# ScalarE's scans of weight rows are put behind the first rounding of the loop's weights in a hybrid encoder layer

## The chip, the core and the metric

The kernel runs on one core of a Trainium2 chip. A core has a matrix engine, TensorE (PE in the profile, with its weight loads as PEld); three engines for elementwise work, VectorE (DVE), ScalarE (ACT) and GpSimd (POOL); and SyncE (SP), which here only issues transfers. All work at the same time, each on its own queue of instructions in a fixed order, and wait for each other by semaphores. Data lie in the on-chip memory, in tiles of 128 partitions; matrix products are written to a separate accumulator memory (PSUM). The metric is the time of one launch in microseconds on the device; lower is better.

## The reference

The reference computes one encoder layer for 1024 tokens of width 1024 in 32-bit floating point. A normalised input goes through one projection into two mixers (windowed grouped-query attention, and a two-dimensional neighbourhood attention); their outputs are normalised, concatenated and projected. What matters here is the second half, a gated block with a short convolution:

```python
hn = rmsnorm(h, norm_ffn)
g = einsum('bsd,df->bsf', hn, w_gate)          # 1024 -> 2816
u = einsum('bsd,df->bsf', hn, w_up)
g = conv3(g) * conv_w + conv_b                 # depthwise, over the tokens
h = h + einsum('bsf,fd->bsd', silu(g) * u, w_down)
out = rmsnorm(h, norm_final)
```

## The kernel before

The 2816 hidden columns are cut into 22 units of 128, taken in an order `FO`. For each unit the products with the gate and the up weights are formed together by a Strassen-like scheme: seven products of half size, named `p1` to `p7` in the class `Gated`, of weight blocks and their sums ("11", "12", "s1" to "s4", "22") with activations prepared once. Each product is made in 16-bit parts: a 32-bit operand is rounded to a 16-bit value `whi`, and what the rounding lost is kept as `wlo`. `group` (lines 1173 to 1177) then issues three matrix instructions for each of four depth blocks, `whi` twice and `wlo` once, so a product is 12 of them. `split_w` (lines 1145 to 1152) makes the two parts: ScalarE rounds (line 1150), VectorE subtracts (line 1151). Both multiply by a scale, a power of two `m`, so that the values fit 16 bits.

The scale of a unit comes from its weights, so they are read twice. First a **scan**: `scan_rows` (lines 1159 to 1164) loads a whole block of 512 KB (384 KB for some blocks of the down weights) into one of two `scan` buffers, through SyncE's queue, and ScalarE squares it and sums along each row (an activation, and a second short instruction that reads the sum). `settle_scales` (lines 1021 to 1035) takes the row sums of up to four units: VectorE adds gate and up (`wv`, line 1027), TensorE transposes so that all partitions see all rows (`wm`, line 1009), VectorE takes the maximum (line 1011) and turns it into `m` (lines 243 to 245) and its inverse (line 1030). Later `load_raw` loads the same weights again, and `split_w` rounds them with `m`.

The first four units are the **head**. Their products are issued product by product: all four units' `p1` and `p2`, then `p5`, `p6`, `p3`, `p7` and `p4`. While the head runs, ten scans are traced: two for each of the next four units, and two for the one after. At the head's end stands a short loop over its four units: `p4` of each, and with each of them three steps of `Weights`, the object that prepares the next unit's weights. The first three steps are `load` (it settles the scales and loads), `w11` and `w12`, the first two roundings for the first unit of the loop.

The **loop over units** (from line 1594) then runs over the other 18. In each turn it forms the seven products of its unit, and between them its helper `more` takes one step of the next unit's `Weights` and one step of `scanning`. The latter are the loop's scans: two for the unit five places ahead, and two of the 24 scans of the down weights, whose scale is needed at the end of the loop. In all there are 60 scans: ten in the head and 50 in the loop.

After the loop the products with the down weights follow, by the same scheme, and then the final normalisation.

What sets the order of the work: TensorE's instructions are kept in the order in which the program lists them. Those of the other engines, and the transfers, are ordered when the kernel is built, by a planner that simulates the engines: of the instructions whose inputs and buffers are ready in its simulation it takes the one of highest priority, normally the one listed first. `tc.high_priority(offset=...)` moves an instruction ahead in that. It can therefore put an instruction of a later turn of the loop well ahead of where it is listed, where an engine is free in its simulation. Once built, each queue's order is fixed. `behind(names)` adds an edge of order, without a semaphore, that puts an instruction later in its engine's queue than the marked one.

## Time and profile before

| What | Value |
|---|---|
| median of 3 runs | 1040.5 us (1039.18 to 1040.81) |
| profiled execution | 1043.51 us |
| its span, first to last instruction | 1041.7 us |
| mean granted TensorE clock | 0.994 |
| TensorE busy | 1014.5 us (97%) |
| VectorE busy | 879.5 us (84%) |
| ScalarE busy | 678.3 us (65%) |
| GpSimd busy | 213.2 us (20%) |
| scans on ScalarE | 60, 61.2 us, from 380.1 to 612.7 us |
| transfers | 191.28 MB, mean 184 GB/s |

How to read the lines: in a timeline a line has the start and the length in us, the engine, the line of the kernel, the instruction with what it writes and reads, its count, and in brackets the idle time of its engine before it and what ended that. In the list of waits, a line has who waited for whom, the time in total, the number of times and the longest. In the view by stages a line has the stage and its length, the busy time of each engine in it (PE, PEld, DVE, ACT, POOL, with counts), the granted TensorE clock as a share of full speed, the share of the transfer engines' time that was used, and GB/s; where the view is of one line of the kernel, it has that line's engine alone. In the list of groups a line has the busy time and the mean length of one instruction in ns, then the idle time before them. The lengths of matrix instructions overlap, so their pace is read from their starts.

### The profile page before, as it was taken

The numbers are of one execution on the slowest core, as the hardware profiler recorded it, in microseconds if no ns is written. First come the engines' busy times: TensorE is split into PE (matmuls) and PEld (weight loads), VectorE is DVE, ScalarE is ACT, GpSimd is POOL, SyncE is SP. The second block draws the span as 40 slices with busy tenths as digits, with TensorE's granted clock in tenths as the row PEclk, the third lists the DMA queues.
The fourth block names the chain that finished last, engine by engine and source line by source line (L and its number), as shares of the span: only waits on it lengthen the run. The fifth ranks groups of instructions, "written<-read, shape, count | busy, mean of one in ns | idle before, by whom it ended". The sixth has DMA issues, their size and how long they took to land.

```text
span 1041.7 us, 15699 instructions
## 1 busy us (share of the span) xinstructions
PE 1014.5 (97%) x5098; PEld 577.9 (55%) x5098; DVE 879.5 (84%) x1748; ACT 678.3 (65%) x1243; POOL 213.2 (20%) x341
## 2 busy tenths in 40 slices
PE   8998999999999999999999999999999999999996
PEld 6776777777775545544344444444444444444446
DVE  6689998766898799899898888888888889899875
ACT  7557787767687587778777765445544656555551
POOL 2225455676866301000000000000000000000002
PEclk9999999999999999999999999999999999999998
DMA  9437574776699775564787752323323678877744
GB/s 347 152 93 147 111 131 85 156 166 141 134 179 224 217 271 195 158 189 149 239 260 251 251 185 91 122 91 122 112 101 112 226 258 303 297 247 258 260 152 162
DMA packets 144276, 191.28 MB, mean 184 GB/s; under 512 B 77377, under 2 KB 88641, under 8 KB 144193
## 3 DMA queue, kind: packets, MB, share of 16 engines
q1 hardware_dynamic: 133536, 164.51, 55.4%
q10 hardware_dynamic: 10656, 25.76, 6.4%
q8 instruction: 40, 0.66, 0.3%
q14 instruction: 44, 0.35, 0.1%
HBM read 132.81 MB, written 28.57 MB: 155 GB/s over the span
## 4 chain that ended last, share of the span: by engine, by line
PE 66%; DVE 5%; DMA 4%; ACT 4%; issue 1%; ACTq 0%; POOL 0%; DVEq 0%; POOLq 0%
PE dn L1177 6%; PE dn L1175 6%; PE dn L1176 6%; PE pj L180 6%; PE z L1176 4%; PE z L1177 4%; PE z L1175 4%; PE x L1177 3%; PE x L1176 3%; PE x L1175 3%; PE y L1175 3%; PE y L1176 3%; PE y L1177 3%; PE pj L172 2%; PE pj L174 2%; PE pj L173 2%
## 5 line engine op out<-in xcount | busy, mean ns | idle before, releaser
L1175 PEld LDWEIGHTS <-whi 128*128 128x128 f16 x898 | 88.2, 98 | 103.0 <-ACT whi L1150 2.6
L1177 PEld LDWEIGHTS <-wlo 128*128 128x128 f16 x898 | 88.0, 98 | 102.2 <-issue 0.8
L1176 PEld LDWEIGHTS <-whi 128*128 128x128 f16 x898 | 88.0, 98 | 100.6 <-issue 0.7
L1177 PE MATMUL dn<-xd,wlo 128*128 128x512 f16 (+1 forms) x330 | 120.4, 365 | 0.0
L1176 PE MATMUL dn<-xd,whi 128*128 128x512 f16 (+1 forms) x330 | 120.4, 365 | 0.0
L1175 PE MATMUL dn<-xd,whi 128*128 128x512 f16 (+1 forms) x330 | 120.4, 365 | 0.0
L172 PE MATMUL pj<-xgh,whi 128*128 128x512 f32 x248 | 107.3, 433 | 0.7 <-ACT whi L156 0.7
L1175 PE MATMUL z<-hg,whi 128*128 128x512 f16 x264 | 100.1, 379 | 0.0
L1176 PE MATMUL z<-hg,whi 128*128 128x512 f16 x264 | 100.1, 379 | 0.0
L1177 PE MATMUL z<-hg,wlo 128*128 128x512 f16 x264 | 100.1, 379 | 0.0
L174 PE MATMUL pj<-xgh,wlo 128*128 128x512 f32 x248 | 98.3, 396 | 1.4 <-POOL wlo L157 1.4
L466 ACT ACTIVATE p<-p,nm 128x385 f32<-128x385 f32 (+3 forms) x128 | 74.7, 584 | 38.0 <-DVE nm L462 33.3
L173 PE MATMUL pj<-xgl,whi 128*128 128x512 f32 x248 | 97.9, 395 | 0.0
L1150 ACT ACTIVATE whi<-ws,m 128x512 f16<-128x512 f32 (+1 forms) x96 | 65.6, 708 | 33.9 <-DVE ws L1316 26.4
L1151 DVE SCALAR_TENSOR_TENSOR wlo<-ws,m,whi 128x512 f16<-128x512 f32 (+1 forms) x96 | 70.1, 739 | 17.6 <-ACT whi L1150 17.4
L1031 POOL TENSOR_TENSOR back<-back,cst 128x4 f32<-128x4 f32 (+1 forms) x7 | 2.3, 335 | 362.4 <-DVE back L1030 362.4
L1164 ACT ACTIVATE scan<-scan 128x1024 f32<-128x1024 f32 (+1 forms) x60 | 61.2, 1019 | 18.8 <-DMA scan<-in_w_down_dram 8.9
L1151 DVE SCALAR_TENSOR_TENSOR wlo<-raw,m,whi 128x512 f16<-128x512 f32 (+1 forms) x78 | 55.1, 730 | 7.4 <-ACT whi L1150 7.4
L1175 PE MATMUL y<-hg,whi 128*128 128x512 f16 x160 | 60.9, 381 | 0.0
L1176 PE MATMUL y<-hg,whi 128*128 128x512 f16 x160 | 60.8, 380 | 0.0
L1177 PE MATMUL y<-hg,wlo 128*128 128x512 f16 x160 | 60.6, 379 | 0.0
L1578 DVE SCALAR_TENSOR_TENSOR xd<-xd,m 128x512 f16<-128x512 f32 x77 | 55.0, 745 | 6.0 <-ACT xd L1577 6.0
(291 smaller groups left out, 2458.7 us busy)
## 6 DMA issues: line engine op xcount, KB each, us to landing
xd<-x SPq DMA_DIRECT2D x77, 256.0 KB, 5.3
raw<-in_w_down_dram SPq DMA_DIRECT2D x64, 256.0 KB, 3.8
x<-c ACTq DMA_DIRECT2D x22, 512.0 KB, 2.8
scan<-in_w_gate_dram SPq DMA_DIRECT2D x18, 512.0 KB, 4.4
scan<-in_w_up_dram SPq DMA_DIRECT2D x18, 512.0 KB, 4.3
raw<-in_w_gate_dram SPq DMA_DIRECT2D x18, 512.0 KB, 3.5
raw<-in_w_up_dram SPq DMA_DIRECT2D x18, 512.0 KB, 3.5
raw<-in_w_in_dram SPq DMA_DIRECT2D x32, 256.0 KB, 3.3
```

Of the source, the lines that this page charges most:

```text
L172: nc.tensor.matmul(ps, w[0], x[0][:, tsl(h)], start=first, stop=False)
L173: nc.tensor.matmul(ps, w[0], x[1][:, tsl(h)], start=False, stop=False)
L174: nc.tensor.matmul(ps, w[1], x[0][:, tsl(h)], start=False, stop=last)
L180: nc.tensor.matmul(ps, a, b, start=i == 0 and b is x[h][0] and a is w[0], stop=i == len(ws) - 1 and a is w[1])
L466: nc.scalar.activation(p[:, 0:e], p[:, 0:e], AF.Exp, bias=nm, scale=-1.0, accum_out=sm)
L1150: nc.scalar.activation(hi, src, AF.Copy, scale=by)
L1151: nc.vector.scalar_tensor_tensor(lo, src, by, hi, op0=ALU.mult, op1=ALU.subtract)
L1164: nc.scalar.activation(t, t, AF.Square, accum_out=dst)
L1175: nc.tensor.matmul(ps, w[0], x[0], start=first and i == 0, stop=False, skip_group_check=True)
L1176: nc.tensor.matmul(ps, w[0], x[1], start=False, stop=False, skip_group_check=True)
L1177: nc.tensor.matmul(ps, w[1], x[0], start=False, stop=last and i == len(ws) - 1, skip_group_check=True)
L1578: nc.vector.scalar_tensor_tensor(lo, t[:, HALF:S], by, hi, op0=ALU.mult, op1=ALU.subtract)
```

## The change

The second rounding of the loop's first unit (`w12`, the last of the three steps taken in the first turn of the short loop at the head's end) is remembered as `first`. From then on, `scan_rows` puts ScalarE's squaring behind it in ScalarE's queue. The ten scans traced in the head are traced before the mark is set and carry no such edge; the 50 of the loop do. The edge is one of order in ScalarE's queue only. Instructions and transfers are the same.

```diff
             hi = fpool.tile([128, n, 128], F16, name="whi", tag="wh", bufs=9, padded_shape=pad)
             lo = fpool.tile([128, n, 128], F16, name="wlo", tag="wl", bufs=9, padded_shape=pad)
-            nc.scalar.activation(hi, src, AF.Copy, scale=by)
+            mark["whi"] = nc.scalar.activation(hi, src, AF.Copy, scale=by)
             nc.vector.scalar_tensor_tensor(lo, src, by, hi, op0=ALU.mult, op1=ALU.subtract)
...
             with behind(*["unit"] * ("unit" in mark)):
                 nc.sync.dma_start(t, src)
-            nc.scalar.activation(t, t, AF.Square, accum_out=dst)
+            with behind(*["first"] * ("first" in mark)):
+                nc.scalar.activation(t, t, AF.Square, accum_out=dst)
...
             u.p4()
             with tc.high_priority(offset=200):
                 w_next.step(3)
+            if i == 0:
+                mark["first"] = mark["whi"]
             if i < 2:
                 units[i + 2].conv()
```

## The prediction

> **What bounds the kernel now.** I read the page first, for the engine that sets the time.

> ```profile
> PE 1014.5 (97%) x5098; PEld 577.9 (55%) x5098; DVE 879.5 (84%) x1748; ACT 678.3 (65%) x1243; POOL 213.2 (20%) x341
> L1164 ACT ACTIVATE scan<-scan 128x1024 f32<-128x1024 f32 (+1 forms) x60 | 61.2, 1019 | 18.8 <-DMA scan<-in_w_down_dram 8.9
> ```

> TensorE (PE) is busy for 97% of the span, so time can only come from its gaps and from stretches in which its clock is low. ScalarE (ACT) has 60 scans, and before some of them it stands idle until their data land: 18.8 us in all. Then I asked who TensorE waits for from 470 to 640 us, which holds the end of the head and the loop's first units.

> ```profile
> PE x L1175 <- ACT whi L1150: 2.1, 1, 2.1
> PE x L1177 <- DVE wlo L1151: 0.2, 1, 0.2
> ```

> There are two waits and no other. The first is the change's own object: the first product of the loop's first unit waits for the rounded weights `whi`. TensorE's timeline shows the place, and a view by stages gives the granted clock (the column after the engines):

> ```profile
> 495.50 0.38 PE L1176 MATMUL z<-hg,whi 128*128 128x512 f16 x1
> 495.71 0.38 PE L1177 MATMUL z<-hg,wlo 128*128 128x512 f16 x1
> 498.19 0.39 PE L1175 MATMUL x<-hg,whi 128*128 128x512 f16 x1 [2.09 <-ACT whi L1150]
> 498.41 0.38 PE L1176 MATMUL x<-hg,whi 128*128 128x512 f16 x1
> 498.97 0.39 PE L1177 MATMUL x<-hg,wlo 128*128 128x512 f16 x1 [0.18 <-DVE wlo L1151]
> ...
> 500.35 0.63 PE L1176 MATMUL x<-hg,whi 128*128 128x512 f16 x1
> 500.78 0.63 PE L1177 MATMUL x<-hg,wlo 128*128 128x512 f16 x1
> ...
> 503.48 0.38 PE L1175 MATMUL y<-hg,whi 128*128 128x512 f16 x1
> ```

> ```profile
> 490.00:496.00 6.00, 6.00 (x29) 2.55 (x26) 6.00 (x12) 3.62 (x7) 0.00 (x0) 1.00 0.62 203
> 499.50:503.40 3.90, 3.90 (x12) 1.43 (x11) 3.90 (x7) 2.76 (x6) 0.00 (x0) 0.56 0.66 243
> 512.00:612.00 100.00, 100.00 (x467) 45.56 (x465) 88.67 (x129) 77.63 (x129) 1.19 (x5) 1.00 0.75 246
> 612.00:712.00 100.00, 100.00 (x469) 45.85 (x468) 85.58 (x128) 48.04 (x70) 3.48 (x10) 1.00 0.31 109
> ```

> Starts of neighbouring products lie 0.215 to 0.22 us apart at clock 1.00 (495.50 to 495.71) and 0.43 apart in the stage whose clock is 0.56 (500.35 to 500.78). So the gap costs twice: by itself, and by the slow clock behind it. The sum, at 0.216 us a product: the x product was due at 495.93 and started at 498.19, **2.26 us** late. From 498.19 to 503.48 are 15 products (12 of x, 3 of y) in 5.29 us, where 15 x 0.216 = 3.24 would do: **2.05 us** more, of which 0.34 is the wait for `wlo` (498.41 to 498.97 is 0.56) and 1.71 the slow clock. Together **4.31 us** hang on one late rounding. From 512 on TensorE is busy 100 of 100 us.

> **Why `whi` is late.** ScalarE's timeline ahead of it:

> ```profile
> 491.61 1.06 ACT L1164 ACTIVATE scan<-scan 128x1024 f32<-128x1024 f32 x1 [1.24 <-DMA scan<-in_w_down_dram]
> 492.67 1.04 ACT L1385 ACTIVATE cv<-cv 128x1024 f32<-128x1024 f32 x1
> 493.95 1.06 ACT L1164 ACTIVATE scan<-scan 128x1024 f32<-128x1024 f32 x1 [0.25 <-DMA scan<-in_w_gate_dram]
> 496.37 1.06 ACT L1164 ACTIVATE scan<-scan 128x1024 f32<-128x1024 f32 x1 [1.27 <-DMA scan<-in_w_up_dram]
> 497.42 1.32 ACT L1150 ACTIVATE whi<-raw,m 128x512 f16<-128x512 f32 x2
> ```

> The scans stand in the queue ahead of the two roundings, and wait for transfers. The last one, for a later unit's up weights, starts at 496.37 and lets `whi` go at 497.42. The scale `m`, which `whi` also needs, comes from VectorE (DVE):

> ```profile
> 465.90 0.75 DVE L1151 SCALAR_TENSOR_TENSOR wlo<-ws,m,whi 128x512 f16<-128x512 f32 x1 [2.14 <-ACT whi L1150]
> 471.70 0.75 DVE L1151 SCALAR_TENSOR_TENSOR wlo<-ws,m,whi 128x512 f16<-128x512 f32 x1 [1.31 <-ACT whi L1150]
> 491.83 0.68 DVE L1011 TENSOR_REDUCE m<-wm 128x4 f32<-128x512 f32 x1
> 495.02 0.16 DVE L245 TENSOR_SCALAR m<-m 128x4 f32<-128x4 f32 x1
> 495.14 1.28 DVE L1397 SCALAR_TENSOR_TENSOR c<-c,back,cv 128x1024 f32<-128x1024 f32 x1
> 496.34 0.17 DVE L1030 RECIPROCAL back<-m 128x4 f32<-128x4 f32 x1
> 498.16 1.41 DVE L1151 SCALAR_TENSOR_TENSOR wlo<-raw,m,whi 128x512 f16<-128x512 f32 x2 [1.65 <-ACT whi L1150]
> 503.15 0.74 DVE L1151 SCALAR_TENSOR_TENSOR wlo<-ws,m,whi 128x512 f16<-128x512 f32 x1
> ```

> `m` is done at 495.18 (495.02 + 0.16). So 2.24 us pass between the moment the data allow `whi` and its start, all of it in scans.

> **The change, part by part.** It adds an edge of order on ScalarE alone: each of the loop's 50 scans (60 less the ten traced in the head) comes behind the second rounding of the loop's first unit. No instruction or transfer is added, and an order inside one queue costs no instruction. The head's ten scans keep their places. How many are moved:

> ```profile
> 433.00:498.00 65.00, 24.37 (x44) 1.00 0.56 171
> 498.00:613.00 115.00, 30.43 (x56) 0.99 0.74 246
> ```

> Each scan is two instructions, so 44 in the upper row are 22 scans, the eleventh to the thirty-second: all 22 leave the head, with 24.4 us of ScalarE's time. With only two scan buffers, two of them can be loaded early; the loads of the others on SP's queue move behind the roundings as well.

> (1) *The roundings.* Behind the last `cv` (492.67 + 1.04) ScalarE has nothing left ahead of `whi`, which then starts when `m` is there. Lower bound of the gain: `m` stays at 495.18, `whi` starts at about 495.25, and with the 0.77 us of now (497.42 to 498.19) the product starts at 496.02, 0.09 late. `wlo` would still stand behind VectorE's 495.14 and 496.34 rows, which end at 496.51; with 0.81 from its start to the product (498.16 to 498.97), the third product starts at 497.32 where 496.45 was due, 0.87 late. Gain 4.31 - 0.09 - 0.87 = 3.35, if the clock holds. Then the fourth set of weights, `wlo` of z (503.15, now 1.65 earlier: 501.50 + 0.81 = 502.31), meets a product due at 497.32 + 24 x 0.216 = 502.50: it fits, by 0.2 us. Upper bound: VectorE too is held up in the head, 2.14 + 1.31 us by a `whi` that stood behind scans which waited for transfers; that gone, its queue, otherwise full, reaches row 491.83 up to 3.45 us earlier, `m` is done near 491.7, ahead of TensorE's need, and all 4.31 come back. I take **4.0**, nearer the upper end, since VectorE has no other long wait there and what it does in that stretch has its inputs.

> (2) *Does the clock hold?* Stalls of 0.09 and 0.87 are left at worst. Two other gaps of this trace bracket them:

> ```profile
> 372.29 1.02 PE L180 MATMUL pj<-mg,wo 128*128 128x512 f16 x4 [1.34 <-DVE mg L1123]
> 61.94 0.50 PE L174 MATMUL pj<-xgh,wlo 128*128 128x512 f32 x1 [1.37 <-POOL wlo L157]
> 374.00:378.00 4.00, 4.00 (x21) 1.99 (x20) 4.00 (x8) 4.00 (x8) 0.00 (x0) 1.00 0.80 319
> 64.00:68.00 4.00, 4.00 (x16) 3.23 (x15) 2.99 (x12) 1.09 (x4) 0.49 (x1) 0.72 0.32 99
> 59.83 0.50 PE L172 MATMUL pj<-xgh,whi 128*128 128x512 f32 x1 [0.66 <-ACT whi L156]
> ```

> One gap of 1.34 us left the clock at 1.00; 0.66 and 1.37 within some 2 us (2.03 together) were followed by 0.72. 0.96 lies below both, so I count the clock as full. [...]

> (3) *The moved scans.* 22 scans of 1.1 us join those of the loop. In 115 us the loop now runs 28, 4.1 us each; at that pace the 50 end near 496 + 50 x 4.1 = 701 instead of 613. The cover is the loop's idle ScalarE: 77.6 of 100 us busy with scans at this pace (512 to 612), 48.0 without (612 to 712), and TensorE without a gap in both. The load of the first stage now lasts into the second; transfers rise there from 109 to about 246 GB/s, which the first stage bore. Price **0**. Without that cover it would be 24.4 us.

> (4) *What is late next.* The scales of units nine to twelve need the loop's tenth scan. Their transposes have a fixed place in TensorE's order:

> ```profile
> 552.04 0.60 PE L1009 MATMUL wm<-cst,wv 128*128 128x128 f32 x4
> 491.16 0.15 DVE L1027 TENSOR_TENSOR wv<-w_rows 128x4 f32<-128x4 f32 x1
> ```

> Now `wv` is there 61 us ahead. After the change the tenth scan ends near 496 + 10 x 4.1 = 537, and TensorE asks at 552.04 - 4.3 = 547.7: some 10 us of slack remain. Price 0.

> Sum: 4.0 less. The profiled execution takes 1043.5 (span 1041.7 and 1.8 around it) and becomes 1039.5; it lies 3.0 above the median of the runs, 1040.5, so for them **1036.5**.

> **Rivals.**
> *The clock still falls* (0.13): the gap shrinks but a short stall is left, at `wlo` or at z, where the fit was 0.2 us, and a slow stretch like the present one follows. For it: the 0.72 after only 2.03 us. Against: 1.34 without a fall. Gain 3.35 - 1.71 = 1.6 to 2.6: 1037.9 to 1038.9.
> [...]
> *It doesn't do what it says* (0.07): something else takes the scans' place ahead of `whi`, or the scales arrive 2 us later in a new order of VectorE's queue. The rows speak against it, since only `cv` work is left there. Nothing moves: 1040.5.
> *Slower* (0.12): the scans now start late and their transfers come more slowly than now. From 5.2 us a scan on, the tenth misses 547.7, TensorE stands at the transposes, and every later product with it. At 5.6 us it ends at 552, and behind one queued step of VectorE (1.28) and `wv` (0.15) TensorE goes on near 553.5: 5.8 lost, 1.7 more by the clock, less the 4.0 won: 3.5 slower, 1044.0. For it: waits for transfers before 16 scans, 18.8 us of idleness. Against: the loop has sustained 4.1 with the same two buffers.
> *More than 4.31* (0.06): other waits of the new order fall away, 1035.

> **How the numbers follow.** The forecast case, gain 3.35 to 4.31, has 0.62: 1036.2 to 1037.2, widened by the spread of the runs (1.6) to 1035.4 to 1038. What a measurement of this kernel can tell from no change is about 0.2%, 2.1 us. Faster: 0.62 + 0.06 + half of 0.13, 0.75. Same: the other half and 0.07, 0.13. Slower: 0.12. The range 1034.8 to 1040.9 takes in the forecast, the faster end, the clock rival and a part of the unmoved case, and leaves out the slower one.

> **What would show it.** In the profile after: no scan on ScalarE from about 433 to the two roundings `whi<-raw`, and those at or before 495.3; the wait of x for `whi` below 0.3 us; the granted clock at 1.00 through 499.5 to 503.4; VectorE's waits of 2.14 and 1.31 for `whi` near 466 and 472 smaller; the last scan near 700; no wait of TensorE at the transposes near 548. Wrong it is if a wait of TensorE above 1.3 us stands anywhere between 490 and 830, or if the roundings are early and the slow stretch is still there.

## The result and the profile after

The changed kernel takes 1038.7 us in the median of 12 runs (1037.37 to 1041.06), beside 1041.6 us of the kernel before on the same chip (12 runs, 1039.18 to 1044.6). The medians lie 2.9 us apart. The ratio, which is not simply the quotient of the medians, is 0.9966, 95% interval 0.9953 to 0.998: 3.5 us less, with 2.1 to 4.9 inside the interval. A second measurement on another chip (below) gives 0.998, 0.9968 to 0.9991: 2.1 us less, with medians again 2.9 apart. So it is faster, but by less than the 4.0 us forecast. The forecast time of 1036.5 was low by 2.2 us: 1.1 of that is the median of before, which was 1040.5 in the three runs shown and 1041.6 in these twelve, and 1.1 is the gain, 2.9 between the medians where 4.0 was forecast.

The profiled execution took 1037.95 us, its span 1036.2, its mean granted clock 0.997. From the page of the changed kernel, the engines and the group of scans:

```profile
PE 1011.8 (98%) x5098; PEld 577.6 (56%) x5098; DVE 879.2 (85%) x1748; ACT 677.7 (65%) x1243; POOL 213.8 (21%) x341
L1165 ACT ACTIVATE scan<-scan 128x1024 f32<-128x1024 f32 (+1 forms) x60 | 61.0, 1018 | 19.8 <-DMA scan<-in_w_down_dram 15.0
```

The same work is done in the same busy times. ScalarE still stands idle 19.8 us before scans (18.8 before the change): the waits for the scans' transfers have not gone, they stand elsewhere. TensorE's timeline of the changed kernel, from the transposes of the head's end to the place where the wait for `whi` was, and on to the next transposes:

```profile
486.23 0.60 PE L1009 MATMUL wm<-cst,wv 128*128 128x128 f32 x4
...
494.22 0.38 PE L1178 MATMUL z<-hg,wlo 128*128 128x512 f16 x1
494.43 0.38 PE L1176 MATMUL x<-hg,whi 128*128 128x512 f16 x1
...
497.02 0.38 PE L1176 MATMUL y<-hg,whi 128*128 128x512 f16 x1
...
497.67 0.38 PE L1176 MATMUL y<-hg,whi 128*128 128x512 f16 x1
...
546.23 0.60 PE L1009 MATMUL wm<-cst,wv 128*128 128x128 f32 x4
```

The first product of x starts 0.21 us after the last of z, with no bracket behind it: no wait. From 494.43 to 497.67 are the same 15 products that took 5.29 us before; now they take 3.24, which is 15 x 0.216. To set both kernels side by side, count from the transposes:

```profile
487.72 0.49 PE L1009 MATMUL wm<-cst,wv 128*128 128x128 f32 x3
```

This row is of the kernel before. There the fourth product of y stands 503.48 - 487.72 = 15.76 us behind the transposes, now 497.67 - 486.23 = 11.44: **4.32 us** less, the 4.31 of the prediction's gap and slow clock. The two spans differ by more, 5.5 us. Of the rest, 1.49 lies ahead of the transposes, which this change does not touch (the last section tells where it is from), and -0.3 behind.

ScalarE's and then VectorE's timeline of the changed kernel show how `whi` came early:

```profile
485.61 1.06 ACT L1386 ACTIVATE cv<-cv 128x1024 f32<-128x1024 f32 x1 [1.65 <-DVE cv L1385]
...
490.47 1.33 ACT L1150 ACTIVATE whi<-raw,m 128x512 f16<-128x512 f32 x2 [3.81 <-DVE m L245]
491.71 0.70 ACT L1150 ACTIVATE whi<-ws,m 128x512 f16<-128x512 f32 x1
...
496.70 1.04 ACT L1165 ACTIVATE scan<-scan 128x1024 f32<-128x1024 f32 x1
```

```profile
487.04 0.68 DVE L1011 TENSOR_REDUCE m<-wm 128x4 f32<-128x512 f32 x1
...
490.22 0.15 DVE L245 TENSOR_SCALAR m<-m 128x4 f32<-128x4 f32 x1
490.41 1.28 DVE L1398 SCALAR_TENSOR_TENSOR c<-c,back,cv 128x1024 f32<-128x1024 f32 x1
491.61 0.17 DVE L1030 RECIPROCAL back<-m 128x4 f32<-128x4 f32 x1
491.70 1.38 DVE L1151 SCALAR_TENSOR_TENSOR wlo<-raw,m,whi 128x512 f16<-128x512 f32 x2
```

ScalarE is now idle for 3.81 us and waits for `m`, where before `m` was there first and the rounding waited behind a scan. The roundings start at 490.47 and not at 497.42, and the first scan of the loop only at 496.70. `m` itself is done 490.37 - 486.23 = 4.14 us behind the transposes, where it was 495.18 - 487.72 = 7.46: VectorE came 3.32 us earlier, about the 2.14 + 1.31 that it had waited for ScalarE near 466 and 472. No such wait of VectorE is left between 462 and 472.

The stages after, all engines first, then the scans alone (line 1165; behind the engine's busy time stand the clock, the share of the transfer engines' time that was used, and GB/s):

```profile
498.00:510.00 12.00, 12.00 (x58) 5.42 (x56) 10.18 (x15) 8.97 (x16) 0.00 (x0) 1.00 0.92 317
512.00:612.00 100.00, 100.00 (x467) 45.58 (x466) 88.53 (x128) 78.73 (x131) 1.20 (x5) 1.00 0.76 250
612.00:712.00 100.00, 100.00 (x469) 45.83 (x467) 85.00 (x129) 68.21 (x111) 2.94 (x10) 1.00 0.59 199
```

```profile
433.00:498.00 65.00, 1.14 (x2) 1.00 0.04 17
498.00:675.00 177.00, 53.53 (x98) 1.00 0.77 256
```

The clock is 1.00 where it was 0.56 before. From 512 on, the first 100 us look as before. The second hundred holds the scans that were moved: ScalarE rises from 48.0 to 68.2 us and the transfers from 109 to 199 GB/s, and TensorE stays at 100 of 100.

### The profile page after: what moved, and what is told of

Its sections match the earlier page's. It is cut to its first block, busy times and chain, and to the rows that moved or that the text cites. A ratio compares the mean times of both kernels' runs of the same rounds, so it can differ in the third digit from the quotient of the medians.

```text
span 1036.2 us, 15688 instructions
## 1 busy us (share of the span) xinstructions
PE 1011.8 (98%) x5098; PEld 577.6 (56%) x5098; DVE 879.2 (85%) x1748; ACT 677.7 (65%) x1243; POOL 213.8 (21%) x341
## 4 chain that ended last, share of the span: by engine, by line
PE 71%; DVE 6%; DMA 2%; ACT 1%; issue 1%; POOL 0%; ACTq 0%; DVEq 0%; POOLq 0%
PE pj L180 6%; PE dn L1177 6%; PE dn L1178 6%; PE dn L1176 6%; PE z L1176 5%; PE z L1177 5%; PE z L1178 5%; PE y L1176 4%; PE y L1177 4%; PE y L1178 4%; PE x L1176 4%; PE x L1177 4%; PE x L1178 3%; PE pj L172 2%; PE pj L174 2%; PE pj L173 2%
## 5 line engine op out<-in xcount | busy, mean ns | idle before, releaser
L1176 PEld LDWEIGHTS <-whi 128*128 128x128 f16 x898 | 88.1, 98 | 100.3
L1177 PEld LDWEIGHTS <-whi 128*128 128x128 f16 x898 | 87.9, 98 | 100.2
L1177 PE MATMUL dn<-xd,whi 128*128 128x512 f16 (+1 forms) x330 | 120.4, 365 | 0.1
L1176 PE MATMUL dn<-xd,whi 128*128 128x512 f16 (+1 forms) x330 | 120.4, 365 | 0.0
L172 PE MATMUL pj<-xgh,whi 128*128 128x512 f32 x248 | 106.9, 431 | 0.8 <-ACT whi L156 0.8
L1176 PE MATMUL z<-hg,whi 128*128 128x512 f16 x264 | 100.1, 379 | 0.0
L1177 PE MATMUL z<-hg,whi 128*128 128x512 f16 x264 | 100.1, 379 | 0.0
L174 PE MATMUL pj<-xgh,wlo 128*128 128x512 f32 x248 | 97.8, 394 | 1.4 <-POOL wlo L157 1.4
L1150 ACT ACTIVATE whi<-ws,m 128x512 f16<-128x512 f32 (+1 forms) x96 | 65.8, 708 | 36.1 <-DVE ws L1317 19.2
L1151 DVE SCALAR_TENSOR_TENSOR wlo<-ws,m,whi 128x512 f16<-128x512 f32 (+1 forms) x96 | 70.1, 739 | 19.3 <-ACT whi L1150 19.1
L1165 ACT ACTIVATE scan<-scan 128x1024 f32<-128x1024 f32 (+1 forms) x60 | 61.0, 1018 | 19.8 <-DMA scan<-in_w_down_dram 15.0
L1150 ACT ACTIVATE whi<-raw,m 128x512 f16<-128x512 f32 (+1 forms) x78 | 51.3, 699 | 18.0 <-DMA raw<-in_w_down_dram 11.8
L1151 DVE SCALAR_TENSOR_TENSOR wlo<-raw,m,whi 128x512 f16<-128x512 f32 (+1 forms) x78 | 55.4, 731 | 8.2 <-ACT whi L1150 8.2
L1176 PE MATMUL y<-hg,whi 128*128 128x512 f16 x160 | 60.6, 379 | 0.0
L1177 PE MATMUL y<-hg,whi 128*128 128x512 f16 x160 | 60.6, 379 | 0.0
```

What stands on the lines that cost most here:

```text
L172: nc.tensor.matmul(ps, w[0], x[0][:, tsl(h)], start=first, stop=False)
L174: nc.tensor.matmul(ps, w[1], x[0][:, tsl(h)], start=False, stop=last)
L1150: mark["whi"] = nc.scalar.activation(hi, src, AF.Copy, scale=by)
L1151: nc.vector.scalar_tensor_tensor(lo, src, by, hi, op0=ALU.mult, op1=ALU.subtract)
L1165: nc.scalar.activation(t, t, AF.Square, accum_out=dst)
L1176: nc.tensor.matmul(ps, w[0], x[0], start=first and i == 0, stop=False, skip_group_check=True)
```

## The experiments

Edits are given against the changed kernel unless said otherwise. Nothing of the computation is left out in any of them.

**The same two kernels again.** The changed kernel was timed once more on another chip, and the kernel before was profiled three more times.

> The changed kernel once more, beside the next one. Theory: 3 to 4.5 us less than before in the median, with executions in two or three groups about 1.7 us apart, since the clock also falls by chance behind the waits near 61 us. Rival (the first comparison was lucky): less than 2 us.

The changed kernel: 1038.77 us beside 1041.72, ratio 0.998 [0.9968, 0.9991], less than the 3 to 4.5 us expected, and again no wait of TensorE between 380 and 560 us.

> The kernel before, unchanged, profiled once more. The wait of x for whi should be 2.0 to 2.4 us in every execution. Theory (a gap of 2.26 us sets the clock back for certain): about 0.5 for 3.4 us behind it. Rival (by chance, as behind the 2.1 us of waits near 61 us, where it fell in six of ten profiles): in some executions the clock stays at 1.00 and the gap costs 2.6 us instead of 4.3.

> The same once more: a second look at whether the clock falls behind the gap of 2.26 us. By chance: at least one of three profiles of before (this, the one before it, and the first) shows no slow stretch near 500 us. For certain: all three do.

> The same a third time, so that the clock behind the gap is seen in four profiles of before, with the same two theories.

The three executions of the kernel before took 1045.54, 1040.69 and 1040.67 us. For each of them TensorE's waits from 470 to 560 us, in this order:

```profile
PE x L1175 <- ACT whi L1150: 2.7, 1, 2.7
```

```profile
PE x L1175 <- ACT whi L1150: 0.9, 1, 0.9
PE x L1177 <- DVE wlo L1151: 0.2, 1, 0.2
```

```profile
PE x L1175 <- ACT whi L1150: 1.5, 1, 1.5
PE x L1177 <- DVE wlo L1151: 0.2, 1, 0.2
```

And the last scan ahead of `whi` on ScalarE, of the first and of the third:

```profile
496.95 1.06 ACT L1164 ACTIVATE scan<-scan 128x1024 f32<-128x1024 f32 x1 [1.87 <-DMA scan<-in_w_up_dram]
498.01 1.32 ACT L1150 ACTIVATE whi<-raw,m 128x512 f16<-128x512 f32 x2
```

```profile
493.93 1.06 ACT L1164 ACTIVATE scan<-scan 128x1024 f32<-128x1024 f32 x1 [1.30 <-DMA scan<-in_w_up_dram]
494.98 1.32 ACT L1150 ACTIVATE whi<-raw,m 128x512 f16<-128x512 f32 x2
```

The wait that the change removes is there each time, always behind a scan that waits for its transfer, but it is 0.9 to 2.7 us long and not the 2.0 to 2.4 expected: measured from the transposes, that scan gets its data and starts 7.4 to 9.3 us behind them in the four executions. The clock differs too: it falls in two of the four, behind the waits of 2.1 and 2.7, and stays full behind 0.9 and 1.5. Here is the stage 499.5 to 503 of the first and of the third of the three.

```profile
499.50:503.00 3.50, 3.50 (x11) 1.31 (x11) 3.50 (x6) 2.36 (x5) 0.00 (x0) 0.58 0.83 254
```

```profile
499.50:503.00 3.50, 3.50 (x18) 1.57 (x16) 3.50 (x6) 3.18 (x7) 0.00 (x0) 1.00 0.14 45
```

Measured as above, from the transposes to the fourth product of y, the four executions of the kernel before take 15.76, 16.08, 12.85 and 13.46 us. Against 11.44 undisturbed the loss is 4.32, 4.64, 1.41 and 2.02, **3.1 in the mean**. That lies between the two gains that the ratios give, 3.5 and 2.1, and near the 2.9 between the medians. The prediction took its 4.31 from one execution, and that was one of the costly ones.

**Only the last scans moved.** A count lets the edge begin with the 31st scan; 20 of the 22 moved scans stay in the head, and only the two that stood last ahead of `whi` go behind it.

```diff
-            with behind(*["first"] * ("first" in mark)):
+            mark["n"] = mark.get("n", 0) + 1
+            with behind(*["first"] * ("first" in mark and mark["n"] > 30)):
```

> The edge is put on the scans from the 31st on only (the 21st of the loop); the twenty before it may stay in the head. Theory (the scans that stand directly ahead of the first roundings hold them up): the two late scans with their waits of 0.25 and 1.27 us leave, VectorE's waits of 2.14 and 1.31 us for whi near 466 and 472 stay, so the scale m stays about 7.5 us behind the transposes, whi starts 0.1 us behind m, and x is late by 0.1 to 1.0 us in all, with the clock at 1.00: 3.3 us less than before (lower bound of the prediction), 1 us more than with all 50 scans moved. Rival (all the moved work counts, 22 scans of 1.1 us): with 20 of 22 scans left in the head nearly nothing is won, x waits 1.5 us or more for whi.

1038.46 us beside 1042.38, ratio 0.997 [0.9956, 0.9985]: the whole gain. The profile has no wait of TensorE from 380 to 640. From ScalarE's and from VectorE's timeline:

```profile
494.01 1.33 ACT L1150 ACTIVATE whi<-raw,m 128x512 f16<-128x512 f32 x2 [1.47 <-DVE m L245]
```

```profile
464.96 1.41 DVE L1151 SCALAR_TENSOR_TENSOR wlo<-ws,m,whi 128x512 f16<-128x512 f32 x2 [1.55 <-ACT whi L1150]
470.43 0.75 DVE L1151 SCALAR_TENSOR_TENSOR wlo<-ws,m,whi 128x512 f16<-128x512 f32 x1 [1.00 <-ACT whi L1150]
```

VectorE still waits for ScalarE in the head, 2.55 us in all, and `m` is done 6.58 us behind the transposes (487.34). Yet the first product of x starts when it is due, at 495.55. So the lower bound of the prediction's sum, with `m` not a moment earlier, left 0.96 us; here `m` came 0.88 earlier than in the execution predicted from, and nothing is left. That is about as much as VectorE's waits shrank (2.55 after 3.45). How early `m` comes beyond that is worth nothing here, so the 1 us less that was expected beside the full change did not show.

**Only one scan moved.** The same edit with 31 for 30.

> The edge is put on the scans from the 32nd on only, so that a single scan of those that stood ahead of the roundings is moved; 21 of 22 stay. Theory (it is the place of a scan at the queue's head, not the amount of work): the last scan's wait of 1.27 us and its 1.06 us are what held whi once m was there; the scan before it ended at 495.1, the same moment as m. So whi starts within 0.2 us of m, x is late by less than 0.5 us, the clock stays at 1.00, and the time is within 1 us of the changed kernel, 2 to 4 us below before. Rival (each moved scan counts its share): a gap above 1 us stays and the gain is below 1 us.

1038.97 us beside 1042.0, ratio 0.9976 [0.9964, 0.9988]. ScalarE's timeline:

```profile
490.87 1.06 ACT L1166 ACTIVATE scan<-scan 128x1024 f32<-128x1024 f32 x1 [0.27 <-DMA scan<-in_w_gate_dram]
...
492.31 1.33 ACT L1150 ACTIVATE whi<-raw,m 128x512 f16<-128x512 f32 x2 [0.29 <-DVE m L245]
```

The scan that now stands last is done before `m`; x starts on time again (493.73 with transposes at 485.52, the 8.21 us of the undisturbed order). One scan of 60, in the wrong place of a queue, carried the whole effect. The other 21 were moved for nothing, and did no harm. The margin is small, though: in this execution that scan's instructions end about 0.2 us ahead of `m`.

**One scan buffer in place of two**, to make the loop's scans wait for their transfers.

```diff
-            t = fpool.tile([128, n, 128], F32, name="scan", tag="scan", bufs=2, padded_shape=[128, KT, 128])
+            t = fpool.tile([128, n, 128], F32, name="scan", tag="scan", bufs=1, padded_shape=[128, KT, 128])
```

> The changed kernel with one scan buffer instead of two, so that each scan's load starts only when the scan before it is done. Theory (the slower rival's mechanism exists, with a threshold of 5.2 us a scan): load 4.3 us to land + 1.2 us of scan make 5.5 to 6 us a scan; the loop's tenth scan ends near 496 + 10 x 5.7 = 553, the transposes for units nine to twelve, due about 50 us after the loop's first product, wait 4 to 8 us, and the kernel is 5 to 12 us slower than the changed one. Rival (there is slack that the prediction did not see, or the planner brings the scans of gate and up forward): no wait of TensorE at the transposes, the same time within 2 us.

1077.42 us, ratio to the kernel before 1.0344 [1.0316, 1.0372], some 39 us above the changed kernel, far beyond the 5 to 12 expected. The group of the loop's scans from 500 to 770 us, TensorE's waits from 560 to 860, and a place of ScalarE's timeline ahead of 560:

```profile
L1165 ACT ACTIVATE scan<-scan 128x1024 f32<-128x1024 f32 (+1 forms) x50 | 51.0, 1019 | 72.7 <-DMA scan<-in_w_up_dram 31.3 <-DMA scan<-in_w_down_dram 24.1 <-DMA scan<-in_w_gate_dram 11.9
```

```profile
PE z L1176 <- DVE gs L1372: 7.8, 5, 2.7
PE wm L1009 <- DVE wv L1027: 5.9, 2, 3.5
PE y L1176 <- ACT whi L1150: 1.9, 2, 1.3
```

```profile
538.95 0.84 ACT L1165 ACTIVATE scan<-scan 128x768 f32<-128x768 f32 x1 [3.21 <-DMA scan<-in_w_down_dram]
539.79 0.70 ACT L1150 ACTIVATE whi<-ws,m 128x512 f16<-128x512 f32 x1
```

A scan now takes 5.4 us (from 501.99 to 765.67 for the 50), and ScalarE is idle before scans for 72.7 us. The transposes of units nine to twelve are not late even so (`wv` at 557.99, no wait there); those of the two later sets are, by 2.39 and 3.49. But most of TensorE's waits are of another kind than the prediction's slower rival: `whi` stands behind a scan in ScalarE's queue, and `gs` comes from VectorE, which waits for such roundings, and both come late in the middle of a unit. In the place shown, `whi` follows a scan that had waited 3.21 us for its transfer, and TensorE stands for 3.21 us until 540.56. One more wait, of 3.18 until 396.91, is of the head. From 380 to 1000 us TensorE's waits add up to some 27 us. The clock is at 0.5 in five stretches, 20.5 us in all, behind some of them, which costs half of that again; together this is most of the 39. So the slower mechanism exists, and what it costs was priced far too low, at 3.5 us.

**Each scan of the loop done twice**, to use up the cover.

```diff
             with behind(*["first"] * ("first" in mark)):
+                if "first" in mark:
+                    junk = ...
+                    nc.scalar.activation(junk[:, 0:128 * n], t..., AF.Square, accum_out=dst)
                 nc.scalar.activation(t, t, AF.Square, accum_out=dst)
```

> The changed kernel with each of the loop's 50 scans squared twice: 50 more activations with their reads, 1.13 us each, 56 us of ScalarE's time more in the loop. Theory (the moved scans cost nothing because ScalarE's idle time covers them): ScalarE is near 100 of 100 us busy until the last scan, which ends between 720 and 760; TensorE waits less than 2 us in the loop and the time is within 2 us of the changed kernel. Rival (no cover): up to 56 us slower; if only the first unit is tight, one new wait of 1 to 3 us for whi or for a c of ScalarE near 500 to 515.

1044.31 us, ratio to before 1.0022 [1.0007, 1.0038], some 6 us above the changed kernel, where within 2 was expected. The two stages of the loop:

```profile
512.00:612.00 100.00, 96.82 (x449) 43.50 (x448) 84.16 (x119) 91.96 (x159) 2.04 (x5) 1.00 0.64 216
612.00:712.00 100.00, 99.27 (x464) 45.18 (x462) 85.08 (x126) 89.66 (x157) 4.08 (x10) 1.00 0.64 219
```

Of some 56 us of added ScalarE work (50 scans of 1.1) about 50 are covered. TensorE loses 3.2 us in the first stage, 2.5 of it in one wait that ends at 515.54, where `whi` stands behind a doubled scan that had waited 1.74 us for its transfer. This is the one new wait near 500 to 515 that the rival named. How much of it is the doubling and how much the transfer isn't shown.

**The roundings late by a set amount**, to measure the price of the gap alone. In the changed kernel, three, four or seven spare roundings stand ahead of the loop's first rounding. Their result is not used; it takes one of the nine buffers of `whi`.

```diff
+                if self.f == FO[HEAD]:
+                    spare = fpool.tile([128, 4, 128], F16, name="spare", tag="wh", bufs=9)
+                    for _ in range(4):
+                        with behind(*["spare"] * ("spare" in mark)):
+                            mark["spare"] = nc.scalar.activation(spare, self.g[:, 0:4], AF.Copy, scale=...)
+                with behind(*["spare"] * (self.f == FO[HEAD])):
                     self.put("11", self.g[:, 0:4])
```

> The changed kernel with three spare roundings ahead of the first one of the loop instead of four (0.62 us less). With four, x waited 1.32 and then 1.08 us (2.4 in all within 2 us) and the clock fell to 0.51; here x should wait about 0.7 and wlo about 1.1 us, 1.8 in all. Theory (a threshold near 2 us of idleness): the clock stays at 1.00. Rival (chance of the phase, as for the waits of 0.7 and 1.36 us near 61 us, behind which the clock fell in three of six profiles): it may fall here too, and 1.7 us are lost, or not.

> The changed kernel with four spare roundings of the same size (0.62 us each, results not used) ahead of the first one of the loop, and what the planner puts between them (up to two activations of 1.1 us). whi starts 2.5 to 4.7 us later than in the changed kernel, of which 3.2 us were slack: x waits between 0 and 1.6 us. Theory (the gap itself sets the clock back, but only from about 2 us on): clock 1.00 behind a gap below 1.4 us, time 0 to 1.6 us above the changed kernel. Rival (any gap in the wrong phase does it): the clock falls to about 0.5 for 3.4 us in some executions and not in others, times in two groups 1.7 us apart.

> The changed kernel with seven spare roundings: whi starts some 4 us later than with four (three roundings of 0.62 and one or two activations of 1.1), x waits 3.5 to 5.5 us. The clock falls for certain by every theory; by the one that counts a fixed stretch it is low for 3.4 us again and costs 1.7, by the one in which it depends on the gap's length it is low for longer. Time: 5 to 8 us above the changed kernel.

With three: 1042.8 us, ratio to before 1.0019 [1.0001, 1.0038]; with four: 1042.78, 1.0006 [0.9988, 1.0023]; with seven: 1045.3, 1.0035 [1.0016, 1.0053]. TensorE's waits from 470 to 560 us, with four:

```profile
PE x L1176 <- ACT whi L1150: 1.3, 1, 1.3
PE x L1178 <- DVE wlo L1151: 1.1, 1, 1.1
```

With three, `whi` was on time and one wait of 2.53 for `wlo` took the place of both; so three and four did not make a small and a middle gap, as was meant, but two of 2.5 and 2.4, and the clock that was expected to hold fell in both. Three cost 4.0 us against the changed kernel (1038.77 on that chip), four cost 4.3 against the kernel with the last scans moved (1038.46 on that chip). Put back by itself, a late rounding gives the whole time of the kernel before: the gap is what the change was worth, and no other effect of the moved scans is needed. With seven the gap is 4.51 us, the time some 6.5 us above the changed kernel (5 to 8 expected), and the clock stays low for longer, 13 products:

```profile
500.00:505.50 5.50, 5.34 (x13) 1.84 (x14) 4.18 (x6) 5.06 (x11) 0.00 (x0) 0.50 0.20 44
```

**The waits near 60 us.** A subtraction of the first projection (line 157) goes to VectorE in place of GpSimd; this is an attempt to gain more.

```diff
-                        mark["early"] = True
+                        mark["early"] = False
```

> The changed kernel, and in the attention part one subtraction (the low part of the third weights, line 157, 2.0 us on GpSimd, for which TensorE waits 1.36 us near 61 us) goes to VectorE, where such a one takes about 0.7 us. Theory (the second place with the same fault: a gap and by chance a slow clock): the wait falls below 0.5 us, no slow stretch behind it, 1 to 2.5 us less than the changed kernel. Rival (VectorE is full there, 3.9 of 4 us from 60 to 64, and its queue delays the subtraction or what stands behind it): no gain, or up to 2 us slower.

1038.8 us, ratio to before 0.998 [0.997, 0.999], the same as the changed kernel on that chip, as the rival had it. The wait only changed its name, from GpSimd's `wlo` at 1.4 us to VectorE's, which is busy for 3.9 of 4 us there (60 to 64):

```profile
PE pj L174 <- DVE wlo L157: 1.5, 1, 1.5
```

A third scan buffer was not tried.

## Why the prediction was right

**(1) The roundings.** The mechanism was right in each step: no scan from 433 to 496.7 (the 1.14 us of the upper stage are the loop's first scan, behind the roundings), `whi` at 490.47 (bound: 495.3), no wait for it, VectorE's two waits gone, `m` early. In the profiled execution the upper bound came true, 4.32. What was mis-sized is the term itself: **the 4.31 came from one execution**, and over four it is 1.4 to 4.6, 3.1 in the mean. It holds the wait for a transfer, and the gap that this left differs by up to 1.8 us between executions (0.9 and 2.7); and it holds the slow clock, which came in two of the four. The prediction did say that its profiled execution lay 3.0 us above the median, and took the whole 4.0 off the median all the same; it did not ask whether the gap and the slow clock were part of those 3.0. That the gain came near the forecast owes something to luck: worked out from the mildest of the four executions, the term would have been 1.4. That `m` could stay late and leave 0.96 was not seen; with 20 scans left in the head, `m` came just early enough. The lateness of `m` differs too: 7.46 us behind the transposes in the execution predicted from, 5.3 to 7.1 in the other three. So the reason for a value near the upper end, that VectorE's waits go, was true of `m` and not needed for the gain.

**(2) Does the clock hold?** It did, because no gap was left. The reason given, that 0.96 lies below gaps which did and did not slow the clock, compared sizes of gaps; the last section shows that not only the size decides.

**(3) The moved scans.** Price 0 is borne out: TensorE 100 of 100 in both stages. The last scan was forecast near 701 and starts at 673.6: the loop took 3.6 us a scan, not 4.1; the runs do not show why. The doubled scans show the cover: of 56 us more about 50 went in.

**(4) What is late next.** Nothing. The tenth scan of the loop starts at 532.0 (its end was forecast for 537), `wv` is there at 533.6 and the transposes stand at 546.23: 12.6 us of slack, 10 forecast. VectorE's row of it:

```profile
533.48 0.15 DVE L1027 TENSOR_TENSOR wv<-w_rows 128x4 f32<-128x4 f32 x1
```

**The rivals.** That the clock still falls, with a gain of 1.6 to 4.31 - 1.71 = 2.6: it did not, as there was no gap for it to follow. That the change doesn't do what it says: it does. Slower: it did not come, since the scans did not slow down; with one buffer, where they did, it began in the middle of units, at what else stands in ScalarE's queue, before it reached the transposes, and at 5.4 us a scan it cost some ten times the 3.5 us given. More than 4.31: the profiled execution shows 5.5, but the 1.49 beyond it is of the clock near 60 us and not of the change.

## What to carry to other kernels

Instructions that wait for transfers and are needed late do not belong ahead of a short step that TensorE needs now, in a queue of fixed order: one scan of 1.06 us here held up 1.4 to 4.6 us, and moving that one was enough. A stall that ends with a transfer is sized from several executions, not from one. And waits of TensorE of one or two microseconds are counted together with their neighbours, since a slow clock behind them can cost nearly as much again: 1.71 us here behind a gap of 2.26.

## What the runs showed of the hardware

```profile
60.00:70.00 10.00, 8.63 (x35) 6.93 (x36) 8.44 (x18) 5.48 (x14) 3.24 (x4) 0.83 0.29 90
```

```profile
60.00:70.00 10.00, 8.64 (x43) 7.17 (x43) 9.71 (x25) 5.89 (x16) 3.92 (x7) 1.00 0.33 89
```

This makes, within about 0.2 us, the 1.49 us by which the two profiled executions differ ahead of the change. Where one execution has two such stretches, the times at which they end can be compared. The kernel before, TensorE's timeline at the end of each; the spacing goes from 0.43 over one mixed step (0.33, 0.35) to the full pace:

```profile
66.05 0.50 PE L174 MATMUL pj<-xgh,wlo 128*128 128x512 f32 x1
66.38 0.28 PE L432 MATMUL s<-ka,q 128*128 128x256 f32 x1
...
502.91 0.51 PE L1176 MATMUL y<-hg,whi 128*128 128x512 f16 x1
503.26 0.38 PE L1177 MATMUL y<-hg,wlo 128*128 128x512 f16 x1
```

Splitting the mixed step between both paces puts the ends at 66.28 and 503.18, 436.90 us apart. The granted clock bears it out: the view by stages gives 0.50 from 62.87 to 66.25 and from 499.80 to 503.10, and 1.00 from 66.28 to 69.60 and from 503.20 to 506.60. In the trace's record of that clock, both stretches at 0.50 are 3.413 us long, from 62.85 to 66.26 and from 499.76 to 503.17. Ends read in the same way, with the distance divided by these 3.413 us:

| kernel | ends, us | apart, us | in steps of 3.413 us |
|---|---|---|---|
| before | 66.28, 503.18 | 436.90 | 128.0 |
| before, the execution with the gap of 2.7 | 65.57, 502.47 | 436.90 | 128.0 |
| three spare roundings | 65.88, 502.77 | 436.89 | 128.0 |
| seven spare roundings | 65.33, 505.64 | 440.31 | 129.0 |
| one buffer | 545.27, 644.22 | 98.95 | 29.0 |
| one buffer | 644.22, 705.71 | 61.49 | 18.0 |
| one buffer | 705.71, 733.01 | 27.30 | 8.0 |

The distances are whole numbers of that step to within 0.06 us, and 440.31 is longer than 436.90 by one, 3.41. A slow stretch of the kernel before lasts one step (eight products at 0.427) and costs half of it, the prediction's 1.71. With the grid laid through all 14 profiles by the granted clock, the idle time of TensorE can be summed for each step of it. Behind 18 steps with 1.70 to 3.14 us of idleness the next was slow, and behind all others, with up to 1.66 us, it was not (steps that were slow already are left out, and so are the last 20 us of the kernel, where the clock also fell behind 1.33 and 1.62). The step of 1.66 is of the kernel before itself, in the execution with the gap of 1.5. In the execution that the prediction read, the steps ahead of the two slow stretches have 1.76 and 2.02 us of idleness, and no other has more than 1.46. So in these profiles the line lies between 1.66 and 1.70 us in one step, about half of it, and whether a gap of 2.3 us, or two waits of 2.0 in all, falls into one step or is shared by two is a matter of how the grid lies against the execution. That accounts for the 2.51 us wait behind a doubled scan, after which the clock stayed at 1.00: it lies in two steps, 1.6 and 1.1. It accounts also for the long slow stretch with seven spare roundings, where the step after the idle one is itself idle for 1.36 us and the clock stays low for one more; a rule for how much idleness keeps it low isn't shown by these runs.

This was read out of the traces afterwards; no kernel was run to place a gap on the grid by intent, so the rule fits these 14 profiles and has not been tested beyond them.
